# Seven Strassen products for the last block's up projection, in a hybrid encoder layer on one Trainium2 core

## The chip, the core and the metric

The kernel runs on one core of one Trainium2 chip. The metric is the device time of one execution in microseconds (us), the median of several runs. A trace of one further execution, taken by the hardware profiler, shows when each instruction ran on the core's engines: PE (TensorE, matrix products; PEld is its weight loading), DVE (VectorE), ACT (ScalarE), POOL (GpSimd) and SP (SyncE, which here issues all DMAs, in order, on one queue).

## The reference, cut to what matters

One inference step of one encoder layer: 2,048 prompt tokens and 32 sample tokens, model width 1,024, all in float32. The mixer (stick-breaking attention beside a state-space scan) is followed by an output projection and by a gated feed-forward part, which is what the change touches:

```python
def conv_ffn(h, conv_prev, p):
    gu = h @ p['w_up']                                # 1024 -> 2 * 2816
    gate, up = gu[..., :D_FF], gu[..., D_FF:]
    gate_c, conv_new = causal_dwconv(gate, conv_prev, p['ffn_conv_w'], p['ffn_conv_b'])
    act = jax.nn.gelu(gate_c, approximate=True) * up
    return act @ p['w_down'], conv_new                # 2816 -> 1024

    m, k, v, ... = mixer(rmsnorm(x, p['g_mix_pre']), ...)
    x = x + rmsnorm(m, p['g_mix_post'])
    f, ffn_conv_new = conv_ffn(rmsnorm(x, p['g_ffn_pre']), ffn_conv_prev, p)
    x = x + rmsnorm(f, p['g_ffn_post'])
```

## The kernel before

**Arithmetic.** Features lie on the 128 partitions, tokens along the rows. A float32 matrix is split into a high part (a cast, on ACT) and a low part (the remainder, on POOL or DVE); a product is three matmuls, high by high, high by low, low by high (`dense`, L120). Width 1,024 is eight chunks (k) of 128; 2,816 is 22 chunks (j).

**Blocks and stages.** The tokens are four blocks (`SBS`, L36) of 512, 512, 512 and 544. First `phase_in` makes queries, keys, values and the scan for all blocks. Then `build` (L1215) runs attention block by block (`heads`), and between its steps it feeds PE with the steps of the block before, from a generator (`Tail.stream`, L1117): output projection (`out_units`), residual and norm (`residual`, `split`, `root`), then for each j a gate and an up projection (`up`), and after each group of j's the down projection of the group before (`down`). The last block's stream runs alone, after all attention (`alone`, L1166), with its own PSUM banks: three named "t", and the two "o".

**One j in `up` (L996).** The gate takes 8 chunks x 3 matmuls for each token tile; the last block has two tiles of 272 tokens (`tiles_of`, L56), the others one of 512. Its result is multiplied by the norm's factor r (L1015, L1017), since the tokens were split without r (`split`, L980 to L985, from the residual alone). Three taps of convolution (L1026, L1028), the gelu (L1033 to L1036) and then the product with the up projection (L1045, L1047) follow; the result is split into `ah` and `al` (L1050, L1051) for the down projection. The last block also stores two columns of the gate as the convolution's new history (L1022, L1023) out of the tile that L1033 overwrites.

**The last block's start.** `stream(3)` takes 8 steps of block 2's owed down projection, then projects half a of its tokens, then half b with half a's residual between, then `root(a)`, `residual(b)`, `split(a)`, `split(b)`, `root(b)`, and the other 24 owed steps. `rstd_steps` (L158) turns a sum of squares into r: single-column matmuls (L169), a power on POOL (L188), matmuls that spread it (L200), all in one PSUM bank "u".

**Weights (`weight`, L97).** In block 0 a weight tile is read raw (L109), cast (L110), subtracted (L111), and both parts are stored to DRAM (L114); later blocks read both parts back (L106). The tiles hold eight chunks, three of them in rotation (`WBUFS`), with two raw ones (`RBUFS`). The down weights come for two output columns at a time (L1067). In the last block five weights of the output projection lie in a pool of their own (`wkeep`) for both halves.

**The order** of instructions on each engine is made ahead by a scheduler that simulates the program and takes what is ready, by the order of the program among what is ready; at run time each engine goes through its list in order.

Of the kernel before, what the change touches and what calls it, by code (L numbers as in the profile page):

```python
# [8 lines left out]
F32 = mybir.dt.float32  # L9
# [9 lines left out]
STORE = True  # L19
WBUFS = 3  # L20
RBUFS = 2

P = 128
D = 1024
# [36 lines left out]
class Kernel:  # L61
# [35 lines left out]
    def weight(self, pool, src, n=KC, key=None, tag=None):  # L97

        nc = self.nc
        w = pool.tile([P, 2, KC, P], F32R, name=tag or "w", bufs=1 if tag else self.wbufs)  # L100
        hi, lo = w[:, 0], w[:, 1]
        keys = key if isinstance(key, list) else [key]
        if keys[0] in self.kept:
            m = n // len(keys)
            for i, k in enumerate(keys):
                nc.sync.dma_start(w[:, :, m * i : m * i + m, :].bitcast(F32), self.kept[k][:])  # L106
            return hi, lo
        raw = self.wp.tile([P, KC, P], F32, name="wraw", bufs=RBUFS)
        nc.sync.dma_start(raw[:, :n, :], src)  # L109
        nc.scalar.copy(hi[:, :n, :], raw[:, :n, :])  # L110
        nc.gpsimd.tensor_tensor(lo[:, :n, :], raw[:, :n, :], hi[:, :n, :].bitcast(F32), op=ALU.subtract)  # L111
        if key is not None and STORE:
            d = self.kept[key] = self.dp.tile([P, 2, n, P], F32, name="wS_" + "_".join(map(str, key)))
            nc.sync.dma_start(d[:], w[:, :, :n, :].bitcast(F32))  # L114
        return hi, lo
# [4 lines left out]
    def dense(self, ps, w, x, c0, c1, ks=KC, k0=0, first=True, last=True, pin=False):  # L120
        nc = self.nc
        (whi, wlo), (xhi, xlo) = w, x
        at = lambda t, k: t[k] if isinstance(t, list) else t[:, k, :]
        for k in range(ks):
            for i, (l, r) in enumerate(((whi, xhi), (whi, xlo), (wlo, xhi))):
                mm = nc.tensor.matmul(  # L126
                    ps[:, : c1 - c0],
                    l[:, k, :],
                    at(r, k0 + k)[:, c0:c1],
                    start=first and i == 0 and k == 0,  # L130
                    stop=last and i == 2 and k == ks - 1,
# [435 lines left out]
def gate(kn, s, xs, xc, r0, tm):  # L567
# [3 lines left out]
    for c in range(4):  # L571
        w = kn.weight(kn.wp, kn.a["wz"][c])
        for c0, c1 in tiles:
            n = c1 - c0
            ps = kn.po.tile([P, 512], F32, name="o")
            for k in range(KC):
                kn.dense(ps, [t[:, k : k + 1, :] for t in w], xs, c0, c1, ks=1, k0=k, first=k == 0, last=k == KC - 1, pin=s == NSB - 1)
                if len(tiles) == 1 or k % 2:
                    yield
# [317 lines left out]
class Tail:  # L897
# [7 lines left out]
    def __init__(self, kn, att, ctx, pu):  # L905
# [13 lines left out]
        self.owed = None  # L919

# [403 lines left out]
```

## Time and profile before

| what | us |
|---|---|
| median of 3 runs (2933.8 to 2943.42) | 2943.15 |
| span of the profiled execution (no other time of it is known) | 2945.7 |
| of it, before the last block's own stage | 2428 |
| block 0's gate and up weights, first to last raw load | 807 to 1256 |
| first gate matmul of the last block | 2512.5 |
| its last gate and up matmuls | 2893 |

Times are counted from the span's start. Rows of the trace read: start, length, engine, line, operation, output<-inputs, shapes, how many are merged (x2), and in brackets how long the engine had been idle and what released it. A line can be that of a helper: all matmuls of `dense` have L126, so the tile's name tells them apart ("t" and "o" are PSUM banks, "w" weights). Queues have a q: SPq is SP's list of DMAs.

### The profile page before, as it was taken

To read this page: it belongs to the slowest core of one execution; us is meant where nothing else is said; L and a number is where in the kernel's file an instruction comes from. 1 tells how busy PE (TensorE), PEld (TensorE's weight loads), DVE (VectorE), ACT (ScalarE), POOL (GpSimd) and SP (SyncE) were. 2 spreads that over 40 slices of the span, in tenths; PEclk is the share of its full clock that TensorE was granted. 3 is DMA by queue.
4 is the path that set the end of the run, shared out by engine and by line. 5 is a ranking of instruction groups with operands and counts; after the bars stand their busy time and mean duration, and the time that the engine had idled before them with its cause. 6 is when DMAs were issued, how large, how long until landed. Compare 5 with 4: busy or idle time off the path is not lost.

```text
span 2945.7 us, 44837 instructions
## 1 busy us (share of the span) xinstructions
PE 2816.0 (96%) x16699; PEld 2427.4 (82%) x16699; DVE 1696.8 (58%) x2628; ACT 1250.6 (42%) x2534; POOL 1273.1 (43%) x1083
## 2 busy tenths in 40 slices
PE   8999999989889999999999999999999999999997
PEld 6777787977778888888788888978888889899997
DVE  7667576557774555537644455786666652623333
ACT  4344444337665444436433334664444443311111
POOL 4565555435676656547422222553223234511113
PEclk9999999989999999999999999999999999999998
DMA  5646463648677777777555556656554445755555
GB/s 179 183 143 187 145 173 120 173 131 271 223 266 246 267 266 251 271 261 249 194 190 182 179 171 212 247 175 219 179 175 165 167 160 200 242 183 172 170 183 194
DMA packets 251308, 586.36 MB, mean 199 GB/s; under 512 B 66154, under 2 KB 107762, under 8 KB 222546
## 3 DMA queue, kind: packets, MB, share of 16 engines
q1 hardware_dynamic: 251090, 583.49, 59.9%
q8 instruction: 133, 2.18, 0.3%
q14 instruction: 85, 0.70, 0.1%
HBM read 445.70 MB, written 137.69 MB: 198 GB/s over the span
## 4 chain that ended last, share of the span: by engine, by line
PE 74%; DVE 12%; DMA 7%; ACT 2%; issue 2%; POOL 1%; SPq 1%; DVEq 0%; POOLq 0%; ACTq 0%
PE o L126 36%; PE u L126 12%; PE t L126 11%; PE z L821 4%; PE pa L862 4%; PE pt L840 3%; PE o L370 2%; DVE xc L346 2%; DMA acB<-acD 1%; DVE prow L672 1%; DMA w<-wS_out 1%; DVE acB L446 1%; DVE xc L342 1%; DVE x L268 1%; DMA xr<-hS 1%
## 5 line engine op out<-in xcount | busy, mean ns | idle before, releaser
L126 PE MATMUL o<-xhi,w 128*128 128x512 f32 (+2 forms) x3968 | 1047.4, 346 | 30.1 <-ACT xhi L292 7.7
L126 PEld LDWEIGHTS o<-xhi,w 128*128 128x128 f32 x3968 | 698.2, 192 | 124.2 <-ACT xhi L292 7.7
L126 PE MATMUL o<-xlo,w 128*128 128x512 f32 (+2 forms) x1984 | 683.8, 345 | 6.9 <-DVE xlo L278 4.2
L111 POOL TENSOR_TENSOR w<-wraw,w 128x1024 fp32r<-128x1024 f32 (+2 forms) x156 | 369.0, 2366 | 228.2 <-ACT w L110 207.1
L677 POOL TENSOR_TENSOR beta<-beta,prow 128x512 f32<-128x512 f32 (+3 forms) x256 | 255.0, 998 | 429.1 <-DVE prow L672 345.5
L126 PEld LDWEIGHTS o<-xlo,w 128*128 128x128 f32 x1984 | 380.5, 192 | 51.7 <-DVE xlo L278 6.1
L1036 POOL TENSOR_TENSOR y<-y,gb 128x512 f32<-128x512 f32 (+1 forms) x88 | 115.8, 1317 | 544.4 <-ACT gb L1035 544.4
L126 PE MATMUL u<-xhi,w 128*128 128x512 f32 x1056 | 349.4, 398 | 0.0
L126 PE MATMUL o<-ah,w 128*128 128x512 f32 x992 | 342.5, 403 | 3.1 <-DVE f L1082 3.0
L845 DVE TENSOR_TENSOR wt<-pt,wt 128x512 fp32r<-128x512 f32 (+2 forms) x320 | 191.7, 602 | 156.5 <-ACT wt L844 153.9
L672 DVE TENSOR_TENSOR_SCAN prow<-gam,prow,z 128x513 f32<-128x513 f32 x192 | 245.3, 1277 | 61.5 <-ACT beta L670 58.9
L844 ACT CAST wt<-pt 128x512 fp32r<-128x512 f32 (+2 forms) x320 | 167.5, 526 | 208.7 <-PE pt L840 207.1
L126 PEld LDWEIGHTS u<-xhi,w 128*128 128x128 f32 x1056 | 199.1, 189 | 46.6
L126 PEld LDWEIGHTS o<-ah,w 128*128 128x128 f32 x992 | 187.5, 189 | 45.4 <-DVE f L1082 3.9
L669 ACT ACTIVATE gam<-z 128x512 f32<-128x512 f32 (+2 forms) x320 | 173.3, 542 | 95.5 <-PE z L821 69.8
L126 PE MATMUL u<-xlo,w 128*128 128x512 f32 x528 | 209.4, 397 | 0.0
L110 ACT CAST w<-wraw 128x1024 fp32r<-128x1024 f32 (+2 forms) x156 | 155.2, 995 | 124.7 <-PE o L126 91.3
L1028 DVE SCALAR_TENSOR_TENSOR y<-gb,cv,y 128x512 f32<-128x512 f32 (+1 forms) x176 | 160.0, 910 | 69.2 <-ACT y L1026 66.3
L126 PE MATMUL o<-al,w 128*128 128x512 f32 x496 | 196.8, 397 | 0.0
L126 PE MATMUL t<-xhi,w 128*128 128x272 f32 x960 | 189.1, 292 | 1.7 <-DMA w<-wS_out 1.3
L840 PE MATMUL pt<-ident,beta 128*128 128x128 f32 x1088 | 183.2, 279 | 7.7 <-DVE rn_v L178 4.4
L862 PE MATMUL pa<-wt,v 128*64 128x256 f32 (+3 forms) x1152 | 176.2, 283 | 12.5 <-DVE wt L845 6.9
(269 smaller groups left out, 5086.3 us busy)
## 6 DMA issues: line engine op xcount, KB each, us to landing
w<-wS_up SPq DMA_DIRECT2D x132, 1024.0 KB, 4.8
w<-wS_dn SPq DMA_DIRECT2D x72, 768.0 KB, 4.8
wS_up<-w SPq DMA_DIRECT2D x44, 1024.0 KB, 4.8
w<-wS_out SPq DMA_DIRECT2D x39, 1024.0 KB, 6.7
wraw<-wup SPq DMA_DIRECT2D x44, 512.0 KB, 5.8
k<-kS SPq DMA_DIRECT2D x80, 256.0 KB, 4.3
v<-vS SPq DMA_DIRECT2D x80, 256.0 KB, 4.2
wS_dn<-w SPq DMA_DIRECT2D x24, 768.0 KB, 4.5
```

The costliest lines, as they stand in the source:

```text
L110: nc.scalar.copy(hi[:, :n, :], raw[:, :n, :])
L111: nc.gpsimd.tensor_tensor(lo[:, :n, :], raw[:, :n, :], hi[:, :n, :].bitcast(F32), op=ALU.subtract)
L126: mm = nc.tensor.matmul(ps[:, : c1 - c0], l[:, k, :], at(r, k0 + k)[:, c0:c1], start=first and i == 0 and k == 0, stop=last and i == 2 and ...
L669: nc.scalar.activation(g[:, c0:512], z, AF.Sigmoid, scale=-0.125)
L672: nc.vector.tensor_tensor_scan(back(pr), back(g), z[:, 0:1].to_broadcast([P, n + 1]), self.kn.ones[:, 0:1] if prev is None else prev, op0= ...
L677: eng.tensor_tensor(b[:, :n], b[:, :n], pr[:, c0 + 1 : 513], op=ALU.mult)
L821: mm = nc.tensor.matmul(z[:, :n], q[:, P * b : P * b + P], k[:, :n], start=e == 0, stop=e == 1 and kc < s)
L840: mm = nc.tensor.transpose(t[:, P * j : P * j + P], w[:, P * j : P * j + P], kn.ident[:])
L844: nc.scalar.copy(hi, t)
L845: nc.vector.tensor_tensor(lo, t, hi.bitcast(F32), op=ALU.subtract)
L862: nc.tensor.matmul(av[:m, 2 * P * p + c0 : 2 * P * p + 2 * P], v[:, j, :m], wt[:, rest, j, c0:], start=kc == s and p + j + rest == 0, stop ...
L1028: nc.vector.scalar_tensor_tensor(y[:, :W], gb[:, i : i + W], kn.col(wc + i), y[:, :W], op0=ALU.mult, op1=ALU.add)
```

## The change

For the last block alone (`FAST = (3,)`), gate chunk j and up chunk j are computed together (`pair` takes the place of `up`). As a 2 x 2 block product it has the gate and up columns on one side, k 0 to 3 and k 4 to 7 in the middle, and token halves a and b on the other. Seven products of four chunks each take the place of eight, by sums of weights and sums of tokens.

- The sums of weights are made in block 0 on DVE, in the raw tiles, four for each j, and stored to DRAM (`sums`). In the last block they are read, cast and split (`factor`, `divide`); three factors are plain weights and are recalled.
- The sums of tokens are made at the last block's start (`normal`), out of tokens that carry r already: so `split` and `root` are not used there, and r is needed before the first product. Half a is normalized while half b is projected.
- Products 2, 3 and 7 are added in PSUM to the banks of products 1, 5 and 6, after ACT or DVE has read those.
- Weight tiles hold four chunks, six in rotation, with five raw ones; in the last block the pairs' weights rotate through the ten half tiles of `wkeep`. The down weights come for one output column at a time. The residual tiles m0 to m7 are one tile. The scratch for dynamic DMAs is smaller.

```diff
-WBUFS = 3
-RBUFS = 2
+UNIT = 4
+WBUFS = 6
+RBUFS = 5
+FAST = (3,)
...
+    def divide(self, pool, raw, m, key=None, tag=None):
+        w = self.held(pool, tag)
+        hi, lo = w[:, 0, :m, :], w[:, 1, :m, :]
+        nc.scalar.copy(hi, raw[:, :m, :])
+        nc.gpsimd.tensor_tensor(lo, raw[:, :m, :], hi.bitcast(F32), op=ALU.subtract)
...
+    def part(self, src, hi, lo, eng=None):
+        nc.scalar.copy(hi, src)
+        (eng or nc.gpsimd).tensor_tensor(lo, src, hi.bitcast(F32), op=ALU.subtract)
...
+    def normal(self, s, half):
+        r = kn.rstd_narrow(att.tmp, *kn.bank, [self.msq[:, c0:c1]], n, D, stay=True)
+        yield
+        for k in range(KC) if c0 == 0 else (0, 1, 2, 3, 4, 5, 6, 7):
+            nc.vector.scalar_tensor_tensor(
+                M[:, k, c0:c1], M[:, k, c0:c1], kn.col(C_GFFN + k), r[:, :n], op0=ALU.mult, op1=ALU.mult
+            )
+            if c0 == 0 or k >= 4:
+                self.part(M[:, k, c0:c1], hi[k][:, c0:c1], lo[k][:, c0:c1], nc.vector if c0 and k % 2 else None)
+            if c0 == 0:
+                yield
+        if c0 == 0:
+            return
...
+        sub(m12, m12, m11)
+        for k in range(4):
+            self.part(M[:, k, c0:c1], hi[k][:, c0:c1], lo[k][:, c0:c1])
+        raw = []
+        for pool, name, w in ((self.yp, "y", 546), (self.yp, "gb", 548), (self.rp, "ub", 544)):
+            raw.append([pool.tile([P, w], F32, name=name, bufs=2)[:, : 2 * n].rearrange("p (k t) -> p k t", k=2) for _ in range(2)])
+        for i in range(2):
+            k = slice(2 * i, 2 * i + 2)
+            sub(raw[0][i], m22[:, k, :], m12[:, k, :])
+            sub(raw[1][i], raw[0][i], m11[:, k, :])
+            sub(raw[2][i], raw[0][i], m21[:, k, :])
+        t = self.mp.tile([P, KC, 544], F32R, name="m")
...
+                self.part(src[e], h[:, k, :], l[:, k, :], nc.vector)
...
+    def sums(self, j, gate, up):
+        op(a11, a11, a21, ALU.subtract)
+        op(a21, a21, a22, ALU.add)
+        op(a22, a22, a11, ALU.subtract)
+        op(a12, a12, a22, ALU.subtract)
+        return {7: a11, 5: a21, 6: a22, 3: a12}
...
+    def pair(self, s, j, acts):
...
+        for i in (1, 2, 5, 6, 3, 7, 4) if j == 0 else (1, 5, 6, 2, 3, 7, 4):
+            w = self.factor(s, j, i)
+            base = {2: 1, 3: 5, 7: 6}.get(i, i)
+            if base == i:
+                ps[i] = self.bank()
+            b = ps[base]
...
+            if i == 1:
+                nc.scalar.copy(p1, b)
+            elif i == 5:
+                nc.scalar.copy(v, b)
+            elif i == 6:
+                add(t, b, p1)
...
     def up(self, s, j, acts):
...
+        if s == 0 and FAST:
+            for i, t in self.sums(j, *raw).items():
+                d = self.raws[j, i] = kn.dp.tile([P, 4, P], F32, name=f"sS_{j}_{i}")
+                nc.sync.dma_start(d[:], t[:])
...
     def stream(self, s, cat):
...
-        chain = self.residual(s, a)
+        chain = chained(self.residual(s, a), self.normal(s, a) if fast else ())
         for n, _ in enumerate(self.out_units(s, cat, b)):
             yield
-            if n % 4 == 0:
+            if n % 4 == 0 or fast and n % 4 == 2:
                 next(chain, None)
...
+        if fast:
+            for _ in self.normal(s, b):
+                pass
+        else:
+            self.split(s, a)
+            self.split(s, b)
+            self.root(s, b)
```

(p1 and t are the two halves of a "y" tile, u and v those of a "ub" tile. The rest of `pair`, from the convolution on, is that of `up`.)

More of the change, by code (lines that the diff above doesn't have):

```diff
@@ L1 @@
 from contextlib import ExitStack
-from itertools import islice
+from itertools import chain as chained, islice
 import concourse.bass as bass
@@ L18 @@
 LOOK = 2
-STORE = True
-WBUFS = 3
-RBUFS = 2
+UNIT = 4
+WBUFS = 6
+RBUFS = 5
+FAST = (3,)
 P = 128
@@ L109, in weight @@
[L109 to L115, printed above, removed]
+        out = []
+        for i in range(0, n, self.unit):
+            m = min(self.unit, n - i)
+            keys = key if isinstance(key, list) else [key and (*key, i)]
+            t = tag and f"{tag}{i}"
+            if keys[0] in self.kept:
+                out += self.recall(pool, keys, m, t)
+            else:
+                out += self.divide(pool, self.raw(src[:, i : i + m, :], m), m, keys[0], t)
```

245 lines of the change are left out of this document (183 added, 62 removed).

## The prediction

> **What bounds the kernel now.** I read the page's engine table first, then the chain of work in order of time for the last token block, then the busy time by stretches.
>
> ```profile
> span 2945.7 us, 44837 instructions
> PE 2816.0 (96%) x16699; PEld 2427.4 (82%) x16699; DVE 1696.8 (58%) x2628; ACT 1250.6 (42%) x2534; POOL 1273.1 (43%) x1083
> ...
> 2559.75 5.53 DMA w<-wS_up
> ...
> 2657.68 6.03 PE t L126 x48
> ```
> ```profile
> 1100.00:1200.00 100.00, 100.00 (x486) 81.90 (x486) 56.29 (x70) 47.29 (x88) 59.18 (x39) 1.00 0.77 264
> 2560.00:2893.00 333.00, 327.59 (x2595) 327.62 (x2596) 108.62 (x246) 62.35 (x125) 51.51 (x38) 0.99 0.53 181
> ```
> TensorE is the bound almost everywhere. In the last block, which runs alone, 48 matmuls of 272 columns take 6.03 us, so one costs 125.6 ns, and up and down projections follow each other without a gap. The columns of the stretches are length, then busy time of PE, PEld, DVE, ACT, POOL, then clock, DMA share and GB/s: in the last block's 333 us DVE works a third of the time and POOL a sixth, so there is room beside PE. In block 0's up projection (the row at 1100) PE is full as well, and the DMA engines are 77% busy at 264 GB/s.
>
> **The change, part by part.** *Matmuls removed.* A gate and up pair in the last block takes 2 x 2 x 8 x 3 = 96 matmuls now and 7 x 4 x 3 = 84 with seven products of the same 272 columns. Over 22 pairs that is 264 matmuls x 125.6 ns = **33.2 us less**. The down projection keeps its matmuls.
>
> *The start of the last block.* So far the tokens enter the first gate matmuls without the factor r, which is applied behind them. After the change r must be there first.
>
> ```profile
> 2512.50:2560.00 47.50, 46.53 (x364) 45.58 (x364) 35.28 (x67) 15.05 (x35) 28.48 (x31) 1.00 0.68 232
> 2512.51 0.40 PE L126 MATMUL t<-xhi,w 128*128 128x272 f32 x1 [0.28 <-DVE f L1082]
> 2530.72 0.74 PE L200 MATMUL u<-ident,rn_w 128*128 128x128 f32 x6
> 2476.69 3.35 DVE L963 SCALAR_TENSOR_TENSOR m<-m,cv,u 128x272 f32<-128x272 f32 x8 [4.26 <-PE u L200]
> 2449.63 1.65 ACT L769 CAST xhi<-att 128x272 fp32r<-128x272 f32 x4
> 2450.39 2.96 POOL L770 TENSOR_TENSOR xlo<-att,xhi 128x272 fp32r<-128x272 f32 x4
> 2524.09 0.76 POOL L782 TENSOR_TENSOR msq<-msq,xr 128x272 f32<-128x272 f32 x1
> hS<-m SPq DMA_DIRECT2D x16, 136.0 KB, 4.3
> L982 DVE SCALAR_TENSOR_TENSOR xlo<-m,cv,xhi x8: 481/492/770, 2490.7 to 2494.3; 128x272 fp32r<-128x272 f32 x8
> L982 DVE SCALAR_TENSOR_TENSOR xlo<-m,cv,xhi x8: 483/990/1012, 2512.7 to 2521.1; 128x272 fp32r<-128x272 f32 x8
> 1104.07 0.69 DVE L1034 SCALAR_TENSOR_TENSOR gb<-gb,y 128x512 f32<-128x512 f32 x1 [0.76 <-ACT gb L1033]
> ```
> PE's cover ends at 2512.5: there the owed down projection of block 2 is done and the first gate begins. The second half's r is complete only at 2530.7 + 0.7 = 2531.5, because its last sum of squares leaves POOL at 2524.9. I leave r there: the first half's root no longer holds the one PSUM bank "u" in between, but eight more 272-wide splits go to POOL. The scalings overwrite what the residual's stores read; those land 4.3 us after their issue, before r. The 16 scaled casts and the two roots' copies that fall away lay beside PE: nothing. Behind r stand, on DVE, eight scalings (3.35 us as L963), two split remainders (about 1) and the 1,088-wide difference (at L1034's 0.69 us for 512, 1.5), then one cast (0.4): product 5 can begin at about 2538. Then come six 544-wide differences (6 x 0.73 = 4.4) and six remainders (4.4) on DVE. Their sources occupy both "y", "gb" and "ub" buffers, which the pair's own copies wait for: product 1's copy until product 6's parts are done, product 5's until part of product 4's is. Product 2 writes product 1's bank and product 3 writes product 5's, so these wait too, and the first pair ends near r + 20 = 2551.5. In the 39 us from 2512.5 PE does this pair's 84 matmuls (10.55 us) and perhaps the next pair's product 1 (1.5): **27 us idle**, less 1 us that this stretch loses now, so 26 us more. From below: with the statistics 5 us earlier and the buffers free in time, 14; from above: all DVE work at the second L982 row's 990 ns instead of the first's 492, some 9 us more, and the statistics 5 us later, 40.
>
> Those two L982 rows are the same instruction with an idle POOL and with a busy one. The Trainium skill (GPSIMD Engine Reference, § 1. Specifications) says that GpSimd shares its SBUF interfaces with VectorE and contends with DVE instructions that have two SBUF inputs; the trace agrees, 492 against 990 ns, and by that rule taken throughout the stall would be 35 us instead of 26. I do not take it throughout, since POOL has only six splits (6 x 0.74) beside 14 us of DVE work.
>
> *A cold TensorE after that idle.*
>
> ```profile
> 2438.55 0.66 PE L126 MATMUL t<-xhi,w 128*128 128x272 f32 x2
> 2479.65 0.41 PE L126 MATMUL t<-xhi,w 128*128 128x272 f32 x2
> 2428.00:2494.40 66.40, 63.71 (x457) 62.07 (x456) 17.28 (x44) 23.13 (x59) 30.10 (x39) 0.92 0.59 217
> ```
> Behind the waits at the block's start two matmuls took 0.66 us instead of 0.41, with the stretch's clock at 0.92: 8% of 66 us is 5 us at most. Most of it lies under waits for DVE: **2 us** (0 to 5).
>
> *The steady pairs.* Of the weights, three factors a pair are recalled in both parts; four are read as raw sums and split again.
>
> ```profile
> 2656.81 0.66 ACT L1033 ACTIVATE gb<-y 128x546 f32<-128x546 f32 x1 [3.73 <-DMA o_fconv<-gb]
> 1097.37 1.30 POOL L1051 TENSOR_TENSOR al<-y,ah 128x512 fp32r<-128x512 f32 x1
> L1050 ACT CAST ah<-y x88: 613/622/650, 897.9 to 2903.6; 128x512 fp32r<-128x512 f32 x66, 128x544 fp32r<-128x544 f32 x22
> ```
> POOL gains 4 x 1.30 + 0.8 = 6 us a pair, ACT 4 x 0.62 + 3 x 0.4 = 3.7. The 333 us stretch holds about 20 of the pairs, so now they do 2.6 and 3.1 us a pair: 8.6 and 6.8 after, in a pair's 10.55 with the down projections as slack between: hidden. DMA reads 3 x 512 + 4 x 256 KB a pair, 2.62 MB, instead of 2.10: 249 GB/s, below the 264 moved in block 0: hidden. New waits are PE's for the bank copies. Each has two products (3.0 us) of cover. ACT stands 3.73 us a pair waiting for the history's DMA, and the next pair's first copy is queued behind that: about 0.2 us a pair, **3 us** (0 to 20).
>
> *The end and one DMA wait.*
>
> ```profile
> 2886.76 6.04 PE t L126 x48
> ```
> ```profile
> PE o L126 <- DMA w<-wS_up: 5.5, 1, 5.5
> ...
> PE t L126 <- ACT ah L1050: 2.1, 1, 2.1
> ...
> PE t L126 <- POOL al L1051: 0.8, 1, 0.8
> ```
> So far the gate's second half (tile t) is the last thing that PE does in a pair, and the activation hangs on it; after the change the gate is complete two products, 3 us, before the pair's end. The 2.1 + 0.8 us before the last down projection go: **2.9 us less** (0 to 2.9). Ten half tiles of look-ahead, filled while PE idles, take the 5.5 us wait: **5.5 us less** (0 to 5.5).
>
> *Block 0 and the half tiles.* What can bind is the raw buffers: a pair holds four of five until its sums have landed in DRAM.
>
> ```profile
> L109 SPq DMA_DIRECT2D wraw<-wup x44: 376/430/2223, 807.3 to 1256.1; - x44
> ```
> ```profile
> 1118.82 0.38 SPq L109 DMA_DIRECT2D wraw<-wup  x1
> 1131.54 0.42 SPq L109 DMA_DIRECT2D wraw<-wup  x1
> v<-vS SPq DMA_DIRECT2D x80, 256.0 KB, 4.2
> vS<-vs SPq DMA_DIRECT2D x32, 256.0 KB, 2.7
> wraw<-wup SPq DMA_DIRECT2D x44, 512.0 KB, 5.8
> ```
> Four DVE sums a pair (0.69 each) take DVE's share from 0.56 to 0.78. Stores of 88 x 256 KB = 23 MB in 449 us are 51 GB/s; full DMA engines would move 264 / 0.77 = 343, so their share rises from 0.77 to 0.92. The raw loop is three issues (1.2), load (4.2), cast and split (1.9), two sums (1.4), issue (0.6), store (2.7) = 12.0 us, against a pair's period of 1131.5 - 1118.8 = 12.7. With loads of 5.8, doubled sums and stores 2 us slower it is 17. Fifteen pairs follow another directly: 0 to 60 us; by the nearest rows it just fits, and I take **3 us**.
>
> The down weights by single columns, the halved recalls and the smaller SBUF scratch I cost at nothing: some 90 more issues of up weights and 104 of down weights on SP, 0.32 and 0.53 us each, 84 us.
>
> ```profile
> L106 SPq DMA_DIRECT2D w<-wS_up x132: 315/320/1421, 1377.8 to 2880.8; - x132
> L106 SPq DMA_DIRECT2D w<-wS_dn x104: 517/530/1130, 1451.2 to 2919.7; - x104
> ```
> ```profile
> SPq L106 <- PE o L126: 475.9, 100, 12.7
> ```
> What hides them is that this queue stands 476 us in waits for matmuls to free the tiles; without that slack the 84 us would be paid.
>
> **Sum.** -33.2 - 5.5 - 2.9 + 26 + 2 + 3 + 3 = -7.6 us on the profiled execution of 2945.7, whose span lies 2.5 above the median of the three runs, 2943.15. Forecast: 2943.15 - 7.6 = **2935.5 us**, no change that a measurement of this kernel can tell (about 0.5%, 14.7 us).
>
> ```profile
> 2508.64 0.79 POOL L967 TENSOR_TENSOR m<-m,xr 128x272 f32<-128x272 f32 x1
> 2509.38 0.75 POOL L782 TENSOR_TENSOR fsq<-fsq,sqt 128x256 f32<-128x256 f32 x1
> ```
> **Rivals.** (1) *The start is covered.* If the statistics come first on POOL, ahead of block 2's squares, which now alternate with them one to one, and the buffers are freed early, the start costs the lower end's 14 and cold 0, the steady pairs and block 0 nothing: -41.6 + 14 = -27.6, **2915.5**. For it: four L967 adds and seven msq sums, 9 us of POOL's work, take from 2508.6 to 2524.9 only because of the alternation. Against it: in the trace they alternate.
> (2) *The raw buffers bind in block 0.* From a loop of 12.7 us on, each us more costs 15. At 14.7 it is +30: 2935.5 + 30 - 3 = **2962.5**, slower. For it: the DMA share of 0.92 and SP's single queue. Against it: the down weights between, and the w tiles' look-ahead.
> (3) *ACT's wait for the history delays the bank copies.* At 1 us in each of 15 direct pairs: +15 - 3, **2947.5**.
>
> **How the numbers follow.** The forecast 0.40, rival 1 0.35, rival 2 0.17, rival 3 0.08. Faster by over 0.5% (below 2928.4) is rival 1: 0.35; slower (above 2957.9) is rival 2: 0.17; the rest 0.48. The range holds rival 1 and reaches into rival 2: 2912 to 2964; the likeliest case's own is 2928 to 2952.
>
> **What would show it.** In the changed profile: 12 matmuls in 1.51 us and 84 in 10.55 between down projections in the last block; a PE idle of some 20 us before the first product 5, released by DVE or ACT, then a clock near half; no wait for w<-wS_up and none before the last down projection; block 0 with PE full and its DMA share above 0.9. I am wrong if block 0 shows PE waiting for POOL's splits of the weights, if the pairs take over 11 us each, or if the first pair starts without a gap.

## The result, and the profile after

The change makes the kernel slower: 2965.66 us (median of four runs) against 2943.28 for four runs of the kernel before, a ratio of 1.0078 (95% interval 1.0057 to 1.0098), 22 us. The forecast was 2935.5, no change, and its range ended at 2964. The profiled execution grew from 2945.7 to 2963.6.

The first two lines of the page, and below them the busy time of four stretches: blocks 0, 1 and 2 and the last block's stage, each from its first read of the scan's output (xlo<-yS), which its output projection starts from, to that of the next. The columns are length, busy PE, PEld, DVE, ACT, POOL, then clock, DMA share and GB/s. The kernel before comes first.

```profile
739.20:1281.50 542.30, 521.33 (x2745) 433.49 (x2744) 314.90 (x425) 289.52 (x578) 343.33 (x258) 0.98 0.76 256
1281.50:1824.90 543.40, 525.83 (x2763) 440.16 (x2762) 293.95 (x421) 216.49 (x475) 182.59 (x189) 0.98 0.59 200
1824.90:2423.20 598.30, 592.03 (x3266) 500.08 (x3265) 397.83 (x541) 292.36 (x634) 224.28 (x229) 0.99 0.55 188
2423.20:2937.50 514.30, 496.82 (x3794) 488.56 (x3792) 190.83 (x425) 118.75 (x260) 139.17 (x142) 0.98 0.57 194
```

The changed kernel:

```profile
span 2963.6 us, 46563 instructions
PE 2792.7 (94%) x16435; PEld 2399.5 (81%) x16435; DVE 1834.1 (62%) x2753; ACT 1331.2 (45%) x2780; POOL 1470.7 (50%) x1293
```

```profile
738.10:1288.80 550.70, 527.17 (x2764) 437.48 (x2763) 387.51 (x517) 297.31 (x654) 379.86 (x333) 0.97 0.84 293
1288.80:1833.80 545.00, 525.62 (x2746) 438.96 (x2745) 291.64 (x418) 216.41 (x480) 184.33 (x194) 0.98 0.62 201
1833.80:2434.50 600.70, 593.41 (x3265) 500.66 (x3264) 395.85 (x540) 292.54 (x632) 223.83 (x229) 0.99 0.58 187
2434.50:2955.50 521.00, 469.80 (x3530) 458.01 (x3529) 259.53 (x462) 189.42 (x420) 295.08 (x264) 0.96 0.65 211
```

Blocks 0 and 1 grew from 1085.7 to 1095.7 us, block 2 by 2.4, the last stage by 6.7. In that stage the 264 matmuls of the forecast are gone. PE's busy time fell by 27.0 us (496.8 to 469.8), not by the 33.2 of the forecast, and its idle time rose from 17.5 us (514.3 - 496.8) to 51.2 (521.0 - 469.8). The longest waits of PE in the last stage show where; the columns are the total, the count and the longest:

```profile
PE u L192 <- POOL msq L805: 11.5, 1, 11.5
PE t L150 <- DVE gb L1133: 6.5, 2, 5.0
PE t L150 <- ACT ah L1190: 6.1, 3, 4.7
PE u L223 <- POOL rn_v L211: 5.0, 2, 3.7
PE u L192 <- DVE m L1038: 3.6, 1, 3.6
PE o L150 <- DVE ub L1133: 2.7, 1, 2.7
```

Three lines (msq, rn_v, m) are the start, where r and the token sums are made. The ah line is mostly the end, before the last down projection (4.7). Two (gb, ub) come behind the start: in the first pairs, VectorE's additions to the banks are queued behind block 2's finish, as the changed kernel's list of VectorE shows:

```profile
2555.85 5.74 DVE L1319 SCALAR_TENSOR_TENSOR f<-f,cv,rstd 128x256 f32<-128x256 f32 x8
2561.51 0.43 DVE L1133 TENSOR_TENSOR y<-o,y 128x272 f32<-128x272 f32 x1
...
2572.27 4.41 DVE L1319 SCALAR_TENSOR_TENSOR f<-f,cv,rstd 128x256 f32<-128x256 f32 x6
```

### The profile page after: what moved, and what is told of

Read it like the earlier page. It is cut to its first block, busy times and chain, and to the rows that moved or that the text cites. A ratio compares the mean times of both kernels' runs of the same rounds, so it can differ in the third digit from the quotient of the medians.

```text
span 2963.6 us, 46563 instructions
## 1 busy us (share of the span) xinstructions
PE 2792.7 (94%) x16435; PEld 2399.5 (81%) x16435; DVE 1834.1 (62%) x2753; ACT 1331.2 (45%) x2780; POOL 1470.7 (50%) x1293
## 5 line engine op out<-in xcount | busy, mean ns | idle before, releaser
L150 PE MATMUL o<-xhi,w 128*128 128x512 f32 (+2 forms) x3520 | 964.5, 353 | 31.2 <-ACT xhi L315 8.6
L150 PEld LDWEIGHTS o<-xhi,w 128*128 128x128 f32 x3520 | 629.6, 193 | 127.0 <-issue 11.5
L135 POOL TENSOR_TENSOR w<-wraw,w 128x512 fp32r<-128x512 f32 (+3 forms) x332 | 531.1, 1607 | 324.6 <-ACT w L134 302.6
L150 PE MATMUL o<-xlo,w 128*128 128x512 f32 (+2 forms) x1760 | 621.1, 353 | 5.5 <-DVE xlo L301 3.6
L150 PEld LDWEIGHTS o<-xlo,w 128*128 128x128 f32 x1760 | 339.2, 193 | 50.4 <-DVE xlo L301 5.3
L134 ACT CAST w<-wraw 128x512 fp32r<-128x512 f32 (+3 forms) x332 | 226.0, 683 | 176.4 <-PE o L150 70.3
L1243 POOL TENSOR_TENSOR y<-y,gb 128x512 f32<-128x512 f32 x66 | 87.0, 1318 | 257.4 <-ACT gb L1242 253.8
L150 PE MATMUL t<-ah,w 128*128 128x272 f32 (+1 forms) x768 | 164.4, 302 | 10.8 <-ACT ah L1190 6.1
L693 ACT ACTIVATE beta<-z 128x512 f32<-128x512 f32 (+2 forms) x320 | 172.7, 540 | 0.0
```

The costliest lines, as they stand in the source:

```text
L134: nc.scalar.copy(hi, raw[:, :m, :])
L135: nc.gpsimd.tensor_tensor(lo, raw[:, :m, :], hi.bitcast(F32), op=ALU.subtract)
L150: mm = nc.tensor.matmul(ps[:, : c1 - c0], l, r, start=first and i == 0 and k == 0, stop=last and i == 2 and k == len(w) - 1, **({"skip_gro ...
L693: nc.scalar.activation(b[:, :n], z, AF.Sigmoid, scale=0.125)
L1243: nc.gpsimd.tensor_tensor(y[:, :W], y[:, :W], t, op=ALU.mult)
```

## The experiments

Theory A, from this comparison: the last block's uncovered start is the main loss, with small stalls in the pairs and in block 0. Theory B: the half tiles and their queue cost the time. Neither survived whole; the table has what the runs gave. Runs 3, 4 and 6 leave a part of the computation out, and all others compute everything. Ratios are to the kernel before on the same chip. The stages are those above, the last one counted to the start of PE's last matmul, 1 us less than in the rows. They come from one profiled execution each.

| kernel | ratio (95% interval) | blocks 0+1 | block 2 | last stage |
|---|---|---|---|---|
| before | 1 | 1085.7 | 598.3 | 513.3 |
| changed | 1.0078 (1.0057 to 1.0098) | 1095.7 | 600.7 | 520.0 |
| 1 half tiles alone | 0.9957 (0.9942 to 0.9973) | 1070.4 | 598.9 | 509.2 |
| 2 half tiles, sums in block 0 | 1.0045 (1.0028 to 1.0062) | 1098.1 | 599.8 | 505.3 |
| 3 start free | 1.0058 (1.0038 to 1.0078) | 1098.9 | 599.9 | 502.9 |
| 4 no splits | 1.0035 (1.0020 to 1.0051) | 1098.0 | 599.8 | 499.9 |
| 5 half tiles, stores alone | 0.9988 (0.9974 to 1.0001) | 1080.5 | 600.7 | 505.2 |
| 6 start free and no splits | 0.9950 (0.9933 to 0.9967) | 1095.6 | 602.2 | 481.2 |
| 7 splits on VectorE | 1.0043 (1.0029 to 1.0056) | 1095.4 | 601.4 | 505.6 |
| 8 sums in the last block | 1.0158 (1.0137 to 1.0178) | 1071.4 | 600.0 | 563.5 |
| 9 = 7, statistics on VectorE | 1.0029 (1.0012 to 1.0045) | 1098.1 | 600.2 | 499.3 |
| 10 = 9, sums in blocks 1 and 2 | 0.9975 (0.9960 to 0.9990) | 1085.1 | 597.9 | 501.0 |
| 11 = 2, sums behind the bank | 1.0047 (1.0029 to 1.0065) | 1094.9 | 600.6 | 504.2 |
| 12 = 10, split there too | 0.9994 (0.9981 to 1.0008) | 1092.9 | 594.0 | 502.8 |
| 13 = 2, ten raw buffers | 1.0001 (0.9988 to 1.0013) | 1084.0 | 598.6 | 507.6 |
| 14 = 1, two raw buffers | 1.0100 (1.0082 to 1.0119) | 1111.9 | 599.0 | 507.8 |
| 15 = 10, all sums in block 2 | 1.0001 (0.9988 to 1.0015) | 1085.9 | 599.2 | 502.7 |
| 16 = 15, more cover | 1.0023 (1.0010 to 1.0036) | 1080.1 | 599.4 | 507.8 |
| 17 = 15, tied to block 2 | 0.9992 (0.9980 to 1.0003) | 1069.6 | 615.9 | 501.5 |
| 18 = 1 again | 0.9958 (0.9942 to 0.9975) | 1072.6 | 600.0 | 503.0 |

Runs 1 and 18 are the same kernel: their ratios agree within 0.0001, but the last stage of their profiled executions differs by 6 us, with the stage's clock at 0.98 and 1.00. So 6 us of one stage in one trace say little, and the difference of two ratios is known to about 0.0025, 7 us. (Runs 10 and 15, further down, are a second measure: by their traces they make all sums in the same place, and their ratios differ by 0.0026.)

### What each part costs: runs 1, 2 and 5

```diff
 run 1
-FAST = (3,)
+FAST = ()
 run 2, besides
-        if s == 0 and FAST:
+        if s == 0:
 run 5, besides
-            for i, t in self.sums(j, *raw).items():
+            for i, t in enumerate(raw[0] + raw[1]):
```

> The changed kernel without any Strassen block: half weight tiles, five raw buffers and single-column down weights stay; pairs, sums of weights and normalized tokens are gone. Theory A (the loss is the uncovered start of the last block, plus small stalls that the pairs and block 0's sums bring): within 5 us of the kernel before, 2940 to 2949, with block 0's stage as long as before (543 us) and blocks 1 and 2 some 2 us longer each. Theory B (the half tiles and their queue cost the time, in all blocks): 2955 or more, block 0's stage 548 us or more.

> As the kernel with half tiles only, but block 0 makes the sums of weights and stores them (nobody reads them). Theory A: 6 to 10 us over the half-tiles kernel, all of it in block 0's stage (551 us instead of 543), with PE waiting for VectorE there to read the up projection's one bank. Theory B (half tiles): less than 3 us over the half-tiles kernel. If the raw buffers bound block 0 (the prediction's rival 2): 20 us or more.

> The half-tiles kernel (no Strassen block) whose block 0 stores its four raw tiles of each pair as they are, without any sum: the same 88 stores and the same hold on the raw buffers as with the sums, but none of VectorE's 88 sums. The kernel with sums and stores was 24 us over the half-tiles kernel. If VectorE's sums are the cost (they are queued ahead of its reading of the up projection's one bank): at most 5 us over the half-tiles kernel. If the stores or the raw buffers are the cost (the prediction's rival 2): 15 us or more over it.

Run 1 fell on neither theory's number: the half-tiles kernel, without any Strassen product, is 0.43% faster than before (12.7 us), and in its trace blocks 0 and 1 are 15 us shorter. That buries theory B. It is more than the half tiles: five raw half tiles take the place of two raw whole ones, and the single-column down weights, the one residual tile and the smaller scratch are in it too. No run takes these apart. Run 2 is 0.88% above run 1: making and storing the sums costs 26 us, in the range that was set aside for the raw buffers. The stores alone (run 5) cost 9 of these, between its two expectations. What is left for the Strassen products themselves, changed kernel against run 2, is a loss of 0.33%, 10 us (15 in the last stage). So the 22 us are about -13 + 26 + 10.

### Why the sums cost 26 us: runs 11, 13 and 14

```diff
 run 11: the loop of sums and stores
         wu = halves(NJ + j)
-        (the loop stood here)
...      (up projection, and VectorE's reading of the bank u)
+        (the loop stands here)
         ahi = self.gp.tile(...)
 run 13 (from run 2)
-RBUFS = 5
+RBUFS = 10
 run 14 (from run 1)
-RBUFS = 5
+RBUFS = 2
```

> The kernel without Strassen products but with the sums in block 0 (1.0045 of the kernel before), its sums and stores moved in the program behind the up projection and VectorE's reading of its bank. If the sums cost because they stand ahead of that reading in VectorE's queue: PE's waits for y disappear and the time falls by 8 to 14 us. If it is the load on VectorE and the longer hold of the raw buffers, or the attention that runs ahead in the meantime: within 3 us of it, or slower.

> The kernel without Strassen products but with the sums in block 0 (1.0045 of the kernel before), with ten raw buffers in place of five (without the pairs' token sums there is room). Theory R (the raw buffers, held until the sums are stored, slow block 0's own stream; attention fills PE in the meantime, and block 1 then has less of it to cover its norm's waits): block 0's stage falls from 552 to 540 us or less, with 2720 matmuls or fewer instead of 2763, and the time falls by 10 to 20 us. Theory V (VectorE's load of sums itself): within 4 us of the kernel with five.

> The half-tiles kernel (0.9957 of the kernel before, no sums, no Strassen products) with two raw half tiles in place of five. Theory R: block 0's stream is slowed by the lack of raw buffers alone: its stage again takes 2740 matmuls or more instead of 2674, block 1's PE idles 16 us or more instead of 9, and the time rises by 8 to 25 us. If raw buffers set nothing: within 4 us of the half-tiles kernel.

In run 2 PE waits in block 0 for VectorE to read the bank u (3.3 us in all), and its 88 sums seemed to stand in the way. Moving them behind that reading changed nothing (1.0047 against 1.0045; the waits were 4.5 us). Ten raw buffers in place of five, with the same sums, gave back half: 1.0045 to 1.0001, 13 us. That was the expected time, though its two signs were not met (block 0's stage 545.1 us with 2740 matmuls, where at most 540 and 2720 were expected). Two in place of five, without any sum, cost 42 us. So at least half of the cost is the hold on the raw buffers, the prediction's rival 2. At least, since the queue SPq shows that ten buffers shorten the waits and don't end them: the waits of the raw loads (L114) for stores of sums to land, first of run 2, then of run 13:

```profile
SPq L114 <- DMA sS<-wraw: 34.5, 29, 3.7
```
```profile
SPq L114 <- DMA sS<-wraw: 23.0, 24, 2.1
```

Where the time is lost is less plain. These are blocks 0 and 1 of run 1, then of run 2:

```profile
739.90:1268.80 528.90, 508.22 (x2674) 424.10 (x2673) 290.88 (x409) 287.40 (x626) 346.88 (x325) 0.98 0.77 260
1268.80:1810.30 541.50, 532.61 (x2833) 444.59 (x2832) 307.69 (x438) 227.84 (x508) 192.66 (x202) 1.00 0.63 202
```
```profile
734.10:1286.00 551.90, 525.78 (x2763) 436.09 (x2762) 390.46 (x516) 296.93 (x654) 378.05 (x333) 0.98 0.84 293
1286.00:1832.20 546.20, 525.78 (x2746) 439.08 (x2745) 291.76 (x418) 216.37 (x481) 184.82 (x194) 0.98 0.62 198
```

With the sums PE idles 26.1 us in block 0's stage (551.9 - 525.8) against 20.7, and 20.4 in block 1's against 8.9, although block 1 makes no sums. The matmul counts suggest how: 89 more matmuls were done in block 0's stage, and 87 were then missing in block 1's. Of the 89, 66 are attention's (tiles pa, pt and z), and the same 66 are missing in block 1's. So a delay of block 0's own work costs little there, since attention fills PE, and most of it is paid one block later, where less attention is left to fill. Block 1's longest wait in run 2 is at its very beginning, 5.6 us for the scan's output to be read (xhi<-yS); run 1 has none over 0.2 us there. I only argue this step: run 13 has moved the same attention ahead (2740 matmuls in block 0's stage, nearly as many as run 14's 2750), but has 12.0 us of idle PE in block 1's against run 14's 20.9, so the count doesn't settle it alone.

### What the last block loses: runs 3, 4, 6 and 7

```diff
 run 3
-            for _ in self.normal(s, b):
-                pass
+            self.firsthalf()      # X[1..7] all from half a's xhi, xlo
 run 4, in factor
-        key = ("sum", j, i)
...
-        return kn.divide(self.ring(), kn.raw(self.raws[j, i][:], 4), 4, ...)
+        key = ("up", NJ + j if i in (5, 6) else j, 4 * (i in (3, 6)))
+        return kn.recall(self.ring(), [key], 4, self.slot())
 run 6: both
 run 7, in divide, for the last block's sums
-        nc.gpsimd.tensor_tensor(lo, raw, hi, op=ALU.subtract)
+        nc.vector.tensor_tensor(lo, raw, hi, op=ALU.subtract)
```

> The changed kernel, but all seven products of every pair read the first half's normalized tokens; the second half is not normalized and the token sums are not made (left out of the computation). So no pair waits for the second half's factor r. Theory A: 25 to 35 us less than the changed kernel, 2931 to 2941, and no idle PE of over 5 us between the end of block 2's down projection and the second pair. Theory B: less than 8 us less than the changed kernel, since block 0 and the queues keep their loss.

> The changed kernel, but the products 3, 5, 6 and 7 recall plain weights that are already in two parts in place of the sums of weights (wrong factors): the same matmuls, but no cast on ScalarE and no subtraction on GpSimd for them in the last block, and 4 x 256 KB more to read a pair; block 0 still makes and stores the sums. Theory A with the part that the splits' load delays the pairs' elementwise work: 8 to 14 us less than the changed kernel, 2952 to 2958, the pairs' 10 us of stalls and the end's waits gone. Theory A without that part (the pairs' stalls come from their own bank copies and order): within 3 us of the changed kernel. If the additional reading bound: slower, with PE waiting for DMA.

> Both earlier edits at once: all products read the first half's tokens, and products 3, 5, 6 and 7 recall plain two-part weights (both leave part of the computation out). If start and splits are two separate costs (about 17 and 20 us of the last block's stage): the stage falls from 520 us to 480 to 488, the whole to 27 to 37 us under the changed kernel, that is 5 to 15 us under the kernel before. If they are one cost seen twice (the first pairs' VectorE and GpSimd work in a crowd): the stage stays at 495 or more, at most 22 us under the changed kernel.

> The changed kernel with the last block's subtractions for the four sums of weights of each pair on VectorE in place of GpSimd; the casts stay on ScalarE. Nothing is left out. If it is GpSimd's queue that made the removal of the splits worth 14 us: 8 to 16 us under the changed kernel. If it is ScalarE's casts, or if VectorE's queue is as bad a place: within 4 us of the changed kernel, or over it.

Theory A asked 25 to 35 us of run 3. It gave 0.20%, 6 us (17 in the last stage). Removing the splits gave 13 us (20 in the stage), and both together 38 (39 in the stage). The stages add up (17 + 20), the ratios don't (6 + 13), and run 3's 6 us are within what two ratios can tell; so I go by the stages. Start and splits are two costs of about the same size. Run 7, which leaves nothing out, gets 10 us back (14 in the stage) by moving the subtraction from GpSimd to VectorE.

Where in the last stage PE idles tells the two apart (us; the stage is cut at 78, 126 and 166 us from its beginning and at 62 before its end):

| PE | before | changed | 3 start free | 4 no splits | 6 both | 7 on VectorE |
|---|---|---|---|---|---|---|
| idle, projections | 3.4 | 2.7 | 2.1 | 3.1 | 2.3 | 2.4 |
| idle, r and token sums | 1.1 | 22.7 | 7.7 | 20.0 | 3.3 | 18.9 |
| idle, first pairs | 5.5 | 7.7 | 9.2 | 1.3 | 4.6 | 4.6 |
| idle, steady pairs | 0.0 | 8.6 | 7.3 | 0.9 | 0.0 | 2.8 |
| idle, end | 7.5 | 9.5 | 9.4 | 9.5 | 9.5 | 10.0 |
| busy, whole stage | 496.8 | 469.8 | 468.3 | 466.1 | 462.6 | 468.0 |

The steady pairs, changed kernel and run 4, in the trace's own words:

```profile
2600.50:2893.50 293.00, 284.40 (x2232) 281.20 (x2231) 142.64 (x245) 106.78 (x230) 155.90 (x115) 1.00 0.67 216
2602.80:2875.70 272.90, 272.00 (x2163) 271.62 (x2162) 111.33 (x236) 71.25 (x159) 55.68 (x48) 1.00 0.86 293
```

So without the splits the steady pairs run with PE nearly full, and 9 us of idle go from the start and the first pairs too. What GpSimd does to VectorE is in the groups by line, pairs of the last block. First VectorE and GpSimd of the changed kernel:

```profile
L1177 DVE SCALAR_TENSOR_TENSOR y<-gb,cv,y 128x546 f32<-128x546 f32 x32 | 42.5, 1327 | 10.6 <-ACT y L1175 10.2
L1292 DVE TENSOR_TENSOR f<-t,f 128x272 f32<-128x272 f32 x80 | 34.2, 438 | 42.8 <-PE t L150 42.8
L1185 DVE TENSOR_TENSOR y<-ub,y 128x512 f32<-128x512 f32 x17 | 19.0, 1118 | 24.1 <-POOL y L1184 24.1
L1187 DVE TENSOR_TENSOR y<-ub,y 128x32 f32<-128x32 f32 x17 | 8.6, 504 | 0.0
```
```profile
L135 POOL TENSOR_TENSOR w<-wraw,w 128x512 fp32r<-128x512 f32 x65 | 95.6, 1485 | 79.9 <-ACT w L134 78.6 <-POOL y L1184 1.0 <-POOL w L135 0.2
```

Then VectorE of run 7, with four more subtractions a pair (L135) of its own:

```profile
L135 DVE TENSOR_TENSOR w<-wraw,w 128x512 fp32r<-128x512 f32 x65 | 58.2, 899 | 19.3 <-ACT w L134 17.9 <-DMA wraw<-sS 1.2
L1292 DVE TENSOR_TENSOR f<-t,f 128x272 f32<-128x272 f32 x79 | 34.3, 439 | 44.9 <-PE t L150 44.7
L1177 DVE SCALAR_TENSOR_TENSOR y<-gb,cv,y 128x546 f32<-128x546 f32 x33 | 31.6, 957 | 0.1
L1185 DVE TENSOR_TENSOR y<-ub,y 128x512 f32<-128x512 f32 x17 | 12.2, 718 | 6.6 <-POOL y L1184 6.6
L1187 DVE TENSOR_TENSOR y<-ub,y 128x32 f32<-128x32 f32 x17 | 3.1, 181 | 0.0
```

The convolution's taps (L1177) take 1327 ns beside GpSimd's splits and 957 without, the gelu's product (L1185) 1118 and 718, and its wait for GpSimd falls from 24.1 us to 6.6. The additions that read a PSUM bank (L1292) take 438 and 439: of these rows only those with two SBUF inputs suffer.

### Putting the pieces right: runs 8, 9, 10, 12, 15, 16, 17 and 18

```diff
 run 8: no sums in block 0; in pair
+        self.here = self.sums(j, four raw tiles of wup[j], wup[NJ + j])
 run 9 (from run 7), residual of half b
-            eng = nc.vector if c % 2 else nc.gpsimd
+            eng = nc.vector if c % 2 or lone else nc.gpsimd   # the squares' sums too
 run 10 (from 9), at the end of up; sums by GpSimd
+        if FAST and s == 1 + j % 2:        # run 15: s == 2
+            raw = [[kn.raw(kn.a["wup"][c][:, i : i + UNIT, :], UNIT) ...]]
+            for i, t in self.sums(j, *raw).items():
+                nc.sync.dma_start(d[:], t[:])  # run 12: kn.divide(kn.wp, t, 4, ("sum", j, i))
 run 16 (from 15)
-        yield from islice(owed, 8)
+        yield from islice(owed, 0 if s in FAST else 8)
 run 17 (from 15), ahead of each raw load
+                    nc.gpsimd.tensor_copy(t[:, 0, 0:1], y[:, 0:1])
```

> The changed kernel with the sums of weights made in the last block, from four raw tiles of the input that each pair reads (four more raw buffers there; the same bytes read a pair as before), and none in block 0. Nothing is left out. If the sums in block 0 cost 24 us through block 0 and block 1: the stretch from block 1's to block 3's normed tokens (738 to 1834 in the changed kernel, 1096 us) falls to 1070 to 1074, the last block's stage gains less than 8, and the whole is 16 to 26 us under the changed kernel. If VectorE's sums cost as much in the last block: within 5 us of the changed kernel, its stage 535 us or more.

Run 8, made from the changed kernel, takes block 0's loss away entirely (1071.4 us) and loses more in the last stage, 563.5. There VectorE's 88 sums (L1081, 128x512) stand in the pairs beside GpSimd's splits. In three groups they take 920 to 1137 ns in the mean, not far from the 1028 of the changed kernel's block 0, and the first group also waits 27.6 us, mostly for raw loads to land. Which of these costs the stage its 43 us, no run separates. This is the slowest of all.

> The kernel with the last block's splits on VectorE, and also the second half's residual additions and its sums of squares on VectorE, which had been idle for 10.6 us while GpSimd alternated these with block 2's squares. Nothing is left out. If GpSimd's order holds r back: PE's wait for GpSimd's msq (11.6 us) falls under 5, and the whole is 6 to 9 us under the kernel with the splits on VectorE. If the wait that follows takes its place (the first half's scalings, block 2's squares, the token sums): less than 3 us under it.

Run 9's gain over run 7 is 0.14%, 4 us, less than asked and less than two ratios can tell; PE's wait for the squares falls from 11.6 us (run 7) to

```profile
PE u L192 <- DVE msq L805: 8.2, 1, 8.2
```

> As the kernel with splits and statistics on VectorE, but the sums of weights are not made in block 0: blocks 1 and 2 read the four raw tiles again for every second j each, GpSimd (a quarter busy there) makes the sums, and they are stored. Nothing is left out. If the sums cost block 0 what they did because VectorE and the stores are near their limits there: the stretch from block 1's to block 3's normed tokens falls from 1095 us to 1070 to 1076, block 2's stage stays at 600 to 604, and the whole is 18 to 26 us under the kernel with statistics on VectorE, 10 to 25 us under the kernel before. If they cost wherever they are: within 8 us of the kernel with statistics on VectorE.

> As the kernel with the sums in blocks 1 and 2, and these also cast and split there (ScalarE, GpSimd) and stored in two parts, so that the last block recalls them: 1 MB more to read a pair there, no cast and no subtraction. Nothing is left out. If the last block's splits still cost 4 to 8 us on VectorE (505.6 us of stage, against 499.9 us without any): 3 to 8 us under the kernel with the sums in blocks 1 and 2. If the additional transfers or the w tiles that the splits take in blocks 1 and 2 cost as much: no faster than it, with PE waiting for DMA or for w.

> The kernel with splits and statistics on VectorE, with all 88 sums of weights made in block 2 by GpSimd (none in blocks 0 and 1). With half of them there block 2's stage was no longer (597.9 us), while block 1's was 15 us longer than with none. If block 2 has that room for all: blocks 0 and 1 together 1070 to 1074 us, block 2 597 to 606, 8 to 16 us under the kernel that shared them between blocks 1 and 2, and so 3 to 10 us under the half-tiles kernel. If block 2 has it not: its stage 612 or more, and no gain.

Run 10 takes 0.54%, 16 us, off run 9, but blocks 0 and 1 come down only to 1085.1 us, not to the 1070 to 1076 that were expected. Run 12's additional splitting gains nothing. Run 15 was no test of block 2. Its raw loads, on SPq:

```profile
1350.00 0.92 SPq L114 DMA_DIRECT2D wraw<-wup  x1
...
1688.01 0.33 SPq L114 DMA_DIRECT2D wraw<-wup  x1
```
```profile
1470.00:1520.00 50.00, 49.71 (x255) 41.18 (x255) 30.67 (x38) 24.32 (x52) 31.77 (x29) 1.00 0.98 344
```

They wait for nothing but a raw buffer, so the scheduler had put all 88 into block 1 (1271 to 1828), where the DMA engines' share then reaches 0.98 (the row above; 0.91 from 1350 to 1690). Run 10's shared sums had gone the same way: all 88 of its raw loads lie between 1349 and 1694 us (DMA share 0.88 from 1350 to 1750, against 0.60 in run 1). So none of its sums were in block 2, as run 15's expectation took them to be, and runs 10 and 15 differ in little but their ratios' noise.

> As the kernel meant to have all sums in block 2, whose trace showed the raw loads all pulled forward into block 1 (1350 to 1688 us, DMA engines 96% busy there), since nothing held them back. Here GpSimd first writes one column of each raw tile out of block 2's activation of that j, so that each load waits for block 2 to reach its j. Nothing is left out. If block 2 has room for the sums: blocks 0 and 1 together 1070 to 1074 us, block 2 598 to 606, the last block's stage 499 to 504; 12 to 20 us under the kernel whose loads ran ahead, and 2 to 10 us under the half-tiles kernel of the same call. If not: block 2's stage 612 or more, and the half-tiles kernel stays the faster.

> The half-tiles kernel without sums and Strassen products once more, beside the kernel with the sums tied to block 2 on the same chip: 0.9957 of the kernel before again, within 0.002.

Tied to block 2, the sums leave blocks 0 and 1 alone (1069.6) but now block 2 is 16 us longer:

```profile
1816.40:2432.30 615.90, 599.11 (x3283) 504.14 (x3281) 418.99 (x542) 293.32 (x634) 356.98 (x398) 0.99 0.77 254
```

Here VectorE is 68% busy (419 of 615.9) and the DMA engines 77%; PE idles 16.8 us, against 7.4 in run 1. VectorE has one instruction more than in run 1 (542 against 541) but 23 us more of busy time (419.0 against 396.0). So placing the sums by GpSimd in block 1 or 2 cost about as much either way (15 and 17 us of these stages over run 1), and a last stage of 501.5 us is no better than run 18's 503.0 without Strassen products. On the same chip the half-tiles kernel beats it, 2930.36 against 2939.11 us.

> As the kernel with all sums in block 2, and the last block's stream no longer takes 8 of block 2's 32 owed steps at its beginning, but all 32 behind the projections, where the second half's r is being made: 24 matmuls of 512 columns, 5.6 us of PE's work, move behind. If the start's idle time is a lack of cover: 4 to 6 us less idle there, and 3 to 6 us under the kernel with all sums in block 2. If the beginning needs these steps as cover for its own loads: within 2 us of it, or slower.

Run 16 moved 5.6 us of cover behind, and the wait for msq did fall by 5.2, to

```profile
PE u L192 <- DVE msq L805: 3.2, 1, 3.2
```

but waits at the stage's beginning rose (2.7 us for the attention's own squares, 1.9 for w<-wS_out), and the kernel came out 0.22% above run 15, no gain. Cover was moved, not made.

## Why the prediction was wrong

**Matmuls, -33.2.** Right: 264 fewer, and in run 6, where little idles, PE's busy time in the last stage is 34.2 us under the old one (496.8 to 462.6). That stage is 24 us shorter than run 2's.

**The start, +26, and a cold TensorE, +2.** Right in place; the start's size came out by luck, and the cold TensorE's was too small. These are the changed kernel's start on PE; in brackets stands the idle time before:

```profile
2535.85 1.15 PE L192 MATMUL u<-ones,msq 128*128 128x1 f32 x6 [11.47 <-POOL msq L805]
2538.31 1.46 PE L223 MATMUL u<-ident,rn_v 128*128 128x128 f32 x6 [1.31 <-POOL rn_v L211]
2543.37 0.98 PE L192 MATMUL u<-ones,fsq 128*128 128x1 f32 x4 [3.60 <-DVE m L1038]
2544.95 0.82 PE L150 MATMUL t<-xhi,w 128*128 128x272 f32 x2 [0.59 <-ACT xhi L1024]
...
2578.64 3.06 PE L150 MATMUL t<-m,w 128*128 128x272 f32 x12 [5.01 <-DVE gb L1133]
2586.32 0.60 PE L150 MATMUL o<-xhi,w 128*128 128x272 f32 x1 [2.71 <-DVE ub L1133]
```
```profile
2512.00:2560.00 48.00, 25.30 (x154) 23.08 (x153) 32.77 (x61) 19.41 (x52) 34.38 (x43) 0.75 0.42 132
2560.00:2600.00 40.00, 32.28 (x230) 31.78 (x230) 32.85 (x50) 16.82 (x35) 32.80 (x27) 0.87 0.78 256
```

r is complete at 2538.31 + 1.46 = 2539.8, 105.3 us behind the stage's first read (before: 108.3). PE idles 22.7 + 7.7 = 30.4 us in the two stretches, 29.4 more than the one that the prediction took off. But run 4 has 21.3 there: 9 of the 30.4 go with the splits, and freeing the start takes 17 us off the stage (run 3), not 26. Not foreseen was who is next in VectorE's queue: the last two waits, 7.7 us, lie behind block 2's finish (L1319) and the first pairs' own taps, not behind the token sums, and both waits are gone in run 4. The clock falls to 0.75 and 0.87 in the two stretches, and PE's busy time fell 6.2 us less than 33.2: that is the cold TensorE's price as far as this trace gives one, above the 0 to 5 of the prediction.

**The steady pairs, +3.** This is the step that failed. The 3 us were for rival 3's wait; the splits, GpSimd's 6 us a pair and ScalarE's 3.7, were put at nothing, "hidden" in the pair's 10.55 us, because the busy sums fit. Run 4 prices the splits at 13 us, 20 in the stage, 8 of them as idle PE in the steady pairs. They fit as a sum, but not in time: the splits lie on the same GpSimd that makes the gelu's product (L1184) and the low parts, and they stretch VectorE's instructions beside them. The prediction had the rows for that (492 and 990 ns of the same instruction) and applied them to the start alone. The Trainium skill's rule (GPSIMD Engine Reference, § 1. Specifications) speaks of two SBUF inputs; the trace agrees, with L1177 and L1185 stretched and L1292, which reads PSUM, not.

**ACT's wait for the history (rival 3).** Not seen: PE's waits for ScalarE's bank copies come to under 2.5 us.

**The end, -2.9.** Wrong in sign, by a misreading. The gate is not the last thing that PE does in the old pair: the row quoted for it (2886.76, t x48) was followed by the up projection's 48 matmuls, 6 us of cover for the activation. They write the banks o, and PE's share of the old kernel's stretch with these tiles alone is

```profile
2892.60:2898.90 6.30, 6.19 (x48) 6.00 (x48) 0.00 (x0) 0.00 (x0) 1.00 0.49 167
```

So the old kernel's last up matmuls end at 2898.8, not at 2893 as the table of the time before has it. In the changed kernel the first of the convolution's taps writes the tile that still holds product 1 for product 7's addition, so it starts only at 2914.39, behind that addition:

```profile
2913.85 0.44 DVE L1133 TENSOR_TENSOR ub<-t,y 128x272 f32<-128x272 f32 x1 [1.00 <-PE t L150]
...
2914.39 0.85 ACT L1175 ACTIVATE y<-gb,cv 128x546 f32<-128x546 f32 x1 [1.50 <-DVE ub L1133]
```

The last wait before the down projection is 4.7 us for ah, in place of 2.1 + 0.8, and it was 4.7, 4.6 and 5.2 in runs 4, 6 and 7, whoever splits the weights. The idle time of the stage's last 62 us rose by 2.0 us (7.5 to 9.5).

**The DMA wait, -5.5.** Gone, and the half-tiles kernel does it: run 1 has 1.6 us of such waits left, without a Strassen product.

**Block 0, +3, and half tiles, 0.** The second failed step. Blocks 0 and 1 cost 10 us more, made of two terms that the prediction never had apart: the half-tiles kernel gives 15 us (run 1), and with the sums 25 are lost again (28 in run 2). The raw loop of 12.0 us against a period of 12.7 was called a fit; rival 2 named the mechanism, and run 13 shows it at half of the cost. Rival 2's 2962.5 us lies near the measured 2965.7, but by luck: it put +30 net on block 0, and two thirds of the miss are the last stage.

The forecast lay 7.6 us under the old span and the trace 17.9 above. Of these 25.5 us, 17.3 are the last stage (forecast -10.6, measured +6.7), 7 are blocks 0 and 1, 2.4 block 2 and -1.1 what lies before. By the table of idle times, the last stage's 17.3 are about 6 in the steady pairs, 5 at the end, 4 in slower matmuls and 3 in the rest; the 20 us that run 4 gives for the splits lie in the steady pairs, the first pairs, the start and the slower matmuls together.

What stays open: how much of the sums' other half is VectorE's load and how much the stores' traffic, and why block 1 pays; and which part of the half-tiles kernel brings its 15 us. No run separates these.

## What to carry to other kernels

A helper engine's work is not hidden because its sum fits beside PE: ask which of its instructions the path waits for, and whether it slows a neighbour on the way. Staging buffers that are held through a second use (compute and store) need to be counted by their new hold, and a delay there may be paid a stage later, where the filler has been used up. Before a change of arithmetic is kept, time its refactoring alone: here the half-tiles kernel has the lowest ratio of all these kernels that compute everything (0.9957), and the arithmetic that it was made for cost 36 us on top, nearly three times what it had gained. The best kernel with Strassen's products, run 10 (0.9975), is no faster than it by anything that these runs can tell.

## What was not expected of the hardware

In the changed kernel the 32-column product L1187 took 178 to 1281 ns, 186 in the median, and with GpSimd's splits gone 175 to 186.

```profile
L1187 DVE TENSOR_TENSOR y<-ub,y x17: 178/186/1281, 2607.1 to 2875.3; 128x32 f32<-128x32 f32 x17
```
```profile
L1187 DVE TENSOR_TENSOR y<-ub,y x16: 175/182/186, 2603.8 to 2856.3; 128x32 f32<-128x32 f32 x16
```

The first row is of the changed kernel, the second of run 7. Five of the 17 took 1250 ns or more. Each of these five began while one of GpSimd's splits (L135) ran, and ended within 0.06 us of that split's end; the other 12, of 178 to 188 ns, had no GpSimd instruction beside them. One of the five, with its split:

```profile
2697.82 1.76 POOL L135 TENSOR_TENSOR w<-wraw,w 128x512 fp32r<-128x512 f32 x1
2698.34 1.28 DVE L1187 TENSOR_TENSOR y<-ub,y 128x32 f32<-128x32 f32 x1
```

So it is not slowed in proportion to its size but held up by up to 1.1 us, until the split has ended. The Trainium skill (SBUF — State Buffer, § SBUF: two separate sides) says that the pair of ports that the two share is locked for a whole instruction and the other engine blocks; these rows agree.
